# A decoder layer on one core: the convolution's inverse transform goes ahead of the out-projection's first products

## The chip, the cores and the metric

The kernel runs on one core of one Trainium2 chip. The core has a matrix engine (TensorE, PE in the profile), two engines for elementwise work (VectorE, DVE; ScalarE, ACT), a general one (GpSimd, POOL) and SyncE (SP), which here only starts transfers. Each engine works through its own queue in order; semaphores tie the queues together. Matrix products are written to PSUM, a small memory of eight banks; everything else lies in SBUF.

The metric is the device time of one execution, in microseconds (us). Three runs of the kernel before took 299.83, 300.6 and 301.85 us; the median is 300.6.

## What is computed

One decoder layer on 256 tokens of width 1024, in float32:

```python
h = rms_norm(x, norm1_g)
q, k, v, u = split(h @ w_in)                     # 512 columns each, u has 1024
q, k = rope(rms_norm(q)), rope(rms_norm(k))      # 8 heads of 64
attn = causal_softmax_attention(q, k, v)         # one block of 256 tokens, so plain causal attention
a, g = split(u + glu_b)
c = causal_depthwise_conv(a * sigmoid(g), 31 taps) + dw_b
conv = silu(layer_norm(c))                       # 512 channels
x = x + concat([attn, conv]) @ w_out             # the out-projection, 1024 x 1024
h = rms_norm(x, norm2_g)
x = x + (silu(h @ w_gate) * (h @ w_up)) @ w_down # the FFN, hidden width 2816
```

## The kernel before

**Split operands.** TensorE multiplies a rounded float32 type, so each operand is kept as two parts: hi (rounded) and lo (the rest). A product is three matmuls: hi with hi, hi with lo, lo with hi. In the names of the profile, `wh` and `wl` are hi and lo of weights, `mixh` and `mixl` of the out-projection's input, `yh` and `yl` of the convolution's spectrum. ScalarE makes each hi (a copy into the rounded type), and then VectorE makes the lo (source minus hi).

**The weights** stream in the order in which they are used, as 1 MB blocks (`raw`, four buffers), and are split in pieces of 128 x 1024, two to a block. There are seven buffers each of `wh` and `wl`. `feed(upto)` makes the hi part of pieces up to `upto + 1` and the lo part of those up to `upto`; when the lo of a block's second piece is issued, the load of the block four further on is issued on SP (L179). TensorE uses one piece for four products of the out-projection, so the hi of a piece is made five pieces ahead of its use and the lo four pieces ahead.

**The scheduler.** The order of work on each engine's queue is the order in which the Python program issues it, and a pass at the end fixes that order. Side work is written as generators ("tasks"). `spawn(gen, wait)` puts one on a list with a due time; `step()` runs every task that is due up to its next `yield n`, sets it due again n steps later, and moves the clock `now` on by one. In the input projection a step is made once for each of its 40 units of six matmuls. In the attention's output loop there is a step for every second head. In the out-projection and the FFN `product()` makes a step after each second product, that is after each six matmuls.

**The convolution** is done by a Fourier transform of length 288, as matrix products. A forward transform gives `hf`; VectorE multiplies by the taps' spectrum to get `Y` (three row groups: 128, 128 and 69 rows, the last row being the bias `dw_b`, written by a small DMA). `conv_task` splits `Y` into `yh`, `yl` (L183, L184). The inverse transform gives `cv`, for the two halves of the tokens: two banks of nine matmuls, with the three matmuls of a product at L215, L216 and L217. It is the first part of `ln_task`, and the rest of that task is the layer norm: statistics of `cv` (L559, L560) and `nb` (L564) on VectorE, one step later; `yn` (L569) on ScalarE, three steps after that; two steps after that eight transposes `cT` on TensorE (L580), SiLU to `cs` (L583), and the split of `cs` into rows 4 to 7 of `mixh` and `mixl`.

**The order around the change.** The attention's output loop issues the matmuls `O` (L625, L626) for eight heads. In its first step, `conv_task` issues the splits of `Y`. After heads 3 and 7 the loop issues the split of `O` into rows 0 to 3 of `mixh` and `mixl`. After the loop `ln_task` is spawned, due at once, which means at the next step. SP is given two loads of `x` for the residual (L635). Then come the out-projection's products for k = 0 to 3 (the attention's rows of `mix`; for each k, two token halves and two column halves, 16 products in four banks `po`), with a `feed` ahead of each k. The next 16 products use rows 4 to 7, the convolution's. They are ordered by column half, and each bank is then added to `x`, and transposed (`x2T`) and split for the FFN. The FFN's gate and up products are `fg`, its down products `pd`.

Of the kernel before, what the change touches and what calls it, by code (L numbers as in the profile page):

```python
# [121 lines left out]
def build(nc, tc, t):  # L122
    with ExitStack() as ctx:
        _build(nc, tc, t, ctx)
    keep_order(nc, tc)


def _build(nc, tc, t, ctx):
# [9 lines left out]
    def mm_bank(name, cols=512):  # L138
        return psum.tile([P, cols], F32, name=name, tag="mm", bufs=4)
# [21 lines left out]
    def step():  # L161
        for task in list(tasks):
            while task in tasks and task[0] <= now[0]:
                try:
                    task[0] = now[0] + next(task[1])
                except StopIteration:
                    tasks.remove(task)
        now[0] += 1
# [25 lines left out]
    def feed(upto):  # L194
        last = NB * BW // PIECE - 1
        while len(pieces) <= min(upto + 1, last):
            dst, src, j = new_piece()
            nc.scalar.activation(dst[0], src, AF.Copy)  # L198
            waiting.append((dst, src, j))
        while waiting and waiting[0][2] <= upto:  # L200
            dst, src, j = waiting.pop(0)
            if j >= 40 and j % 4 == 1:
                nc.scalar.activation(dst[1], dst[0].bitcast(F32), AF.Copy, scale=-1.0)  # L203
                nc.gpsimd.dma_start(dst[1].bitcast(F32), src, accum_op=ALU.add)  # L204
            else:
                nc.vector.tensor_tensor(dst[1], src, dst[0].bitcast(F32), op=ALU.subtract)  # L206
            if j % 2:
                load_block(j // 2 + RAW)

    def wtile(col, width):  # L210
        j, c = divmod(col, PIECE)
        return [p[:, c:c + width] for p in pieces[j]]
# [427 lines left out]
    def product(bank, lhs, w, start, stop):  # L640

        for a, (l, r) in enumerate(((lhs[0], w[0]), (lhs[0], w[1]), (lhs[1], w[0]))):
            nc.tensor.matmul(bank, l, r, start=start and a == 0, stop=stop and a == 2)  # L643
        ticks[0] += 1
        if ticks[0] % 2 == 0:
            step()
# [24 lines left out]
        yield 0  # L671

    off = 10 * BW
    for k in range(4):
        feed(off // PIECE + LEAD)
        for i in range(NT):
            for n in range(2):
                if k == 0:
                    po[i, n] = mm_bank(f"po{i}{n}")
                product(po[i, n], [m[:, k, tok(i)] for m in mix], wtile(off + n * W, W), k == 0, False)  # L680
        off += D
# [147 lines left out]
```

## Time and profile before

| | |
|---|---|
| median of three runs | 300.6 us (299.83 to 301.85) |
| the profiled execution | 301.44 us |
| its span, first to last instruction | 299.7 us |
| its mean granted TensorE clock | 0.994 |
| busy: TensorE / its weight loads | 293.0 / 237.2 us |
| busy: VectorE / ScalarE / GpSimd | 166.6 / 168.9 / 26.7 us |
| loaded and stored | 63.89 MB |

All times inside the execution are counted from the first instruction. In a line of the timeline, the first number is the start and the second the length. Then come the engine, the line of the kernel, the operation, output `<-` inputs, sizes and a count. A bracket gives the idle time of that engine before the instruction and what ended it. A matmul's length includes the time until its results have drained, so lengths of neighbours overlap; the distance from start to start is the cost of one in a row. "PEld" is the load of the stationary operand, which runs beside matmuls. The granted clock is the share of its full speed that TensorE was given.

### The profile page before, as it was taken

The page shows a single profiled execution, that of the slowest core. Times are in us where ns is not written, and L with a number is a line of the kernel's source. Part 1 is how long each engine was busy: PE and PEld are TensorE (multiplying, and loading weights), DVE is VectorE, ACT ScalarE, POOL GpSimd, SP SyncE. Part 2 cuts the span into 40 slices and gives each one's busy share as a digit, 9 for nine tenths or more (in the row PEclk, how much of TensorE's full clock was granted, in tenths as well). Part 3 has the DMA queues.
Part 4 walks back from the last instruction along what each step waited for, and adds up shares of the span by engine and source line. Part 5 has one row for each costly group of instructions (what it writes and reads, how often), then busy time and mean ns, then how long its engine had stood idle before and what let it go on. Part 6 is the DMA issues. An engine that isn't in the chain of part 4 may idle for free.

```text
span 299.7 us, 3659 instructions
## 1 busy us (share of the span) xinstructions
PE 293.0 (98%) x1357; PEld 237.2 (79%) x1357; DVE 166.6 (56%) x278; ACT 168.9 (56%) x246; POOL 26.7 (9%) x48
## 2 busy tenths in 40 slices
PE   8999999999799999999999999999999999999995
PEld 6888877777588788888888888888888888888883
DVE  3899986999745857952542542542542644224011
ACT  6776759899515766564654744744744735544200
POOL 0006380000000000001101101101101101101100
PEclk9999999999989999999999999999999999999999
DMA  7999869446505353465795794794695779663312
GB/s 261 415 413 356 316 248 332 143 140 196 228 0 229 116 218 140 142 281 116 256 323 113 263 328 97 269 326 98 271 316 116 270 215 257 245 195 70 71 38 102
DMA packets 12340, 63.89 MB, mean 213 GB/s; under 512 B 1633, under 2 KB 2241, under 8 KB 6562
## 3 DMA queue, kind: packets, MB, share of 16 engines
q1 hardware_dynamic: 9874, 54.86, 49.1%
q0 software_dynamic: 2304, 8.79, 14.6%
q8 instruction: 10, 0.16, 0.2%
q14 instruction: 8, 0.07, 0.1%
q10 hardware_dynamic: 144, 0.00, 0.0%
HBM read 55.26 MB, written 1.05 MB: 188 GB/s over the span
## 4 chain that ended last, share of the span: by engine, by line
PE 87%; DVE 9%; ACT 2%; DMA 1%; issue 0%; SPq 0%; DVEq 0%; ACTq 0%
PE fg L643 40%; PE pd L643 20%; PE p L604 12%; PE po L643 8%; DVE wl L206 3%; PE aT L728 2%; DVE p L473 1%; DMA Y<-dw_b 1%; PE warm L261 1%; DVE sm L456 1%; DVE yl L184 1%; PE cv L215 1%; PE cv L216 1%; PE cv L217 1%; PE x2T L665 1%; DVE ua L500 0%
## 5 line engine op out<-in xcount | busy, mean ns | idle before, releaser
L198 ACT ACTIVATE wh<-raw 128x1024 fp32r<-128x1024 f32 x90 | 93.5, 1055 | 53.0 <-PE fg L643 25.3
L206 DVE TENSOR_TENSOR wl<-raw,wh 128x1024 fp32r<-128x1024 f32 x76 | 91.4, 1222 | 41.2 <-ACT wh L198 41.2
L643 PE MATMUL fg<-wh,g 128*128 128x512 f32 x352 | 111.5, 392 | 0.0
L643 PEld LDWEIGHTS fg<-wh,g 128*128 128x128 f32 x352 | 66.1, 188 | 13.5
L643 PE MATMUL fg<-wl,g 128*128 128x512 f32 x176 | 68.6, 390 | 0.0
L643 PE MATMUL pd<-wh,act 128*128 128x512 f32 x176 | 54.8, 390 | 0.0
L643 PEld LDWEIGHTS pd<-wh,act 128*128 128x128 f32 x176 | 33.0, 188 | 6.8
L643 PEld LDWEIGHTS fg<-wl,g 128*128 128x128 f32 x176 | 33.1, 188 | 6.6
L643 PE MATMUL pd<-wl,act 128*128 128x512 f32 x88 | 34.2, 389 | 0.0
L604 PE MATMUL p<-wh,xh 128*128 128x512 f32 x80 | 32.9, 412 | 0.0
L204 POOL DMA_DIRECT2D wl<-raw x14 | 12.3, 876 | 222.5 <-DVE wl L206 89.8
L604 PE MATMUL p<-wh,xl 128*128 128x512 f32 x80 | 31.3, 391 | 0.0
L604 PE MATMUL p<-wl,xh 128*128 128x512 f32 x80 | 26.5, 392 | 0.0
L732 DVE TENSOR_TENSOR act<-aT,act 128x512 fp32r<-128x512 f32 (+1 forms) x12 | 7.8, 648 | 31.4 <-ACT act L730 31.4
L730 ACT ACTIVATE act<-aT 128x512 fp32r<-128x512 f32 (+1 forms) x12 | 6.8, 563 | 25.2 <-PE aT L728 25.2
L643 PEld LDWEIGHTS pd<-wl,act 128*128 128x128 f32 x88 | 16.5, 188 | 3.4
L604 PEld LDWEIGHTS p<-wh,xh 128*128 128x128 f32 x80 | 15.1, 189 | 3.7 <-issue 0.7
L604 PEld LDWEIGHTS p<-wh,xl 128*128 128x128 f32 x80 | 15.1, 189 | 3.1
L604 PEld LDWEIGHTS p<-wl,xh 128*128 128x128 f32 x80 | 15.1, 189 | 3.0
L721 DVE SCALAR_TENSOR_TENSOR ac<-fg,rstd,sf 128x512 f32<-128x512 f32 (+1 forms) x12 | 8.1, 707 | 12.2 <-PE fg L643 11.6
L203 ACT ACTIVATE wl<-wh 128x1024 fp32r<-128x1024 f32 x14 | 14.7, 1048 | 0.0
L643 PE MATMUL po<-wh,mixl 128*128 128x512 f32 x32 | 13.1, 408 | 1.3 <-DVE mixl L184 1.3
(139 smaller groups left out, 266.4 us busy)
## 6 DMA issues: line engine op xcount, KB each, us to landing
raw<-w SPq DMA_DIRECT2D x45, 1024.0 KB, 5.3
wl<-raw POOLq DMA_DIRECT2D x14, 512.0 KB, 4.6
first<-first SPq DMA_DIRECT2D x8, 384.0 KB, 5.8
xtok<-xtok SPq DMA_DIRECT2D x2, 512.0 KB, 9.1
x<-xtok SPq DMA_DIRECT2D x2, 512.0 KB, 6.8
out<-o SPq DMA_DIRECT2D x4, 256.0 KB, 2.0
inv<-inv POOLq DMA_DIRECT2D x1, 768.0 KB, 7.0
fwd<-fwd POOLq DMA_DIRECT2D x1, 648.0 KB, 4.2
```

The lines of the kernel that those rows point to most:

```text
L184: eng.tensor_tensor(dst[1], src, dst[0].bitcast(F32), op=ALU.subtract)
L198: nc.scalar.activation(dst[0], src, AF.Copy)
L203: nc.scalar.activation(dst[1], dst[0].bitcast(F32), AF.Copy, scale=-1.0)
L204: nc.gpsimd.dma_start(dst[1].bitcast(F32), src, accum_op=ALU.add)
L206: nc.vector.tensor_tensor(dst[1], src, dst[0].bitcast(F32), op=ALU.subtract)
L215: nc.tensor.matmul(out, lhs[0], rhs[0], start=start, stop=False)
L604: nc.tensor.matmul(banks[i], (xh, xh, xl)[a][:, kt, sls[i]], w[a % 2], start=kt == 0 and a == 0, stop=kt == KT - 1 and a == 2 - (order[-1] ...
L643: nc.tensor.matmul(bank, l, r, start=start and a == 0, stop=stop and a == 2)
L721: nc.vector.scalar_tensor_tensor(u[:, :width], banks[i][:, W - width:] if width < W else banks[i], ffn["r"][:, i:i + 1], ffn["s", c][i][:, ...
L728: nc.tensor.transpose(b[:, a, :], ups[i][:, a * P:(a + 1) * P], ident)
L730: nc.scalar.activation(hi, b[:, 0:nf, :], AF.Copy)
L732: nc.vector.tensor_tensor(lo, b[:, 0:nf, :], hi.bitcast(F32), op=ALU.subtract)
```

## The change

One call of `step()` is added ahead of the loop over the out-projection's first 16 products:

```diff
@@ -671,6 +671,7 @@
         yield 0
 
     off = 10 * BW
+    step()
     for k in range(4):
         feed(off // PIECE + LEAD)
         for i in range(NT):
```

`ln_task` is the task that is due there. Its first part, the 18 `cv` matmuls, is issued ahead of the first product instead of behind the second. As the steps after that stay where they are, each later part of the task is issued two products (six matmuls) earlier too: the statistics behind product 2 instead of 4, `yn` behind product 8 instead of 10, and `cT`, `cs` and the split of `cs` behind product 12 instead of 14. Relative to the weights' feeds, which stay at their products, `yn` is now issued ahead of the feed of k = 2 and the `cT` group ahead of the feed of k = 3; each stood behind that feed before.

## The prediction

> **What bounds the kernel now.** I read the page first: is one engine full, and does its clock hold?
>
> ```profile
> span 299.7 us, 3659 instructions
> ...
> PE 293.0 (98%) x1357; PEld 237.2 (79%) x1357; DVE 166.6 (56%) x278; ACT 168.9 (56%) x246; POOL 26.7 (9%) x48
> ...
> PEclk9999999999989999999999999999999999999999
> ```
>
> TensorE (PE) is busy for 98% of the span, and the granted clock dips in one slice of the 40, the twelfth (7.5 us each: 82.4 to 89.9 us). That dip is where the change works. Second, the chain of waits in order of time (start, length, what), around that place:
>
> ```profile
> 77.75 1.89 DVE yl L184 x3
> 79.64 0.61 DVE mixl L184
> 80.25 0.04 issue
> ...
> 87.23 8.17 PE po L643 x36
> 95.40 0.87 PE cT L580 x8
> 96.27 11.73 PE po L643 x48
> 108.01 0.87 PE x2T L665 x8
> 108.88 1.38 PE po L643 x6
> 110.26 4.08 PE fg L643 x18
> ...
> 244.23 51.72 PE pd L643 x228
> ```
>
> At 77.75 the chain leaves TensorE for VectorE (DVE): three subtractions for yl, one for mixl, and only then products. From 110 us to 296 us it is TensorE without a break, 0.227 us for a product's matmul (51.72 / 228, and 8.17 / 36). So whatever TensorE gains before 110.26 should arrive at the end undiminished, unless something feeding it is late. Third, the timeline of TensorE there (start, duration, and in brackets the idle time before and who ended it):
>
> ```profile
> 78.27 0.50 PE L643 MATMUL po<-wh,mixh 128*128 128x512 f32 x1 [0.48 <-ACT mixh L183]
> 78.61 0.40 PE L643 MATMUL po<-wl,mixh 128*128 128x512 f32 x1
> 80.29 0.50 PE L643 MATMUL po<-wh,mixl 128*128 128x512 f32 x1 [1.29 <-DVE mixl L184]
> ...
> 81.17 0.63 PE L643 MATMUL po<-wh,mixl 128*128 128x512 f32 x1
> ...
> 84.50 0.39 PE L216 MATMUL cv<-yl,inv 69*128 69x512 f32 x1
> ...
> 84.96 0.40 PE L215 MATMUL cv<-yh,inv 128*128 128x512 f32 x1
> ...
> 86.84 0.39 PE L217 MATMUL cv<-yh,inv 69*128 69x512 f32 x1
> 87.07 0.39 PE L643 MATMUL po<-wh,mixh 128*128 128x512 f32 x1
> ...
> 95.24 1.03 PE L580 MATMUL cT<-c_ident,yn 128*128 128x128 f32 x8
> ...
> 110.09 0.39 PE L643 MATMUL fg<-wh,g 128*128 128x512 f32 x1
> ```
>
> The attention's last matmul ends at 77.79 (78.27 less 0.48). The first product then waits for ScalarE's mixh, and its third matmul 1.29 us for VectorE's mixl. Then the rhythm is slow: 8 steps from 81.17 to 84.50 take 3.33 us, while the inverse transform's second half (84.96 to 87.07, 9 steps in 2.11) has 0.234 us each. The windows say why (window, its length, busy time of PE, PEld, DVE, ACT and POOL, granted clock, DMA share, GB/s):
>
> ```profile
> 80.00:81.00 1.00, 0.71 (x3) 0.63 (x4) 0.83 (x2) 0.00 (x0) 0.00 (x0) 0.99 0.05 20
> 81.00:82.00 1.00, 1.00 (x4) 0.72 (x3) 0.00 (x0) 0.00 (x0) 0.00 (x0) 0.50 0.00 0
> 84.00:85.00 1.00, 1.00 (x5) 0.78 (x5) 0.00 (x0) 0.00 (x0) 0.00 (x0) 0.80 0.00 0
> ```
>
> The granted clock is 0.50 from about 81.0 to 84.4, right behind the idle time. At 0.234 the 8 steps would take 1.87 us, so half clock costs 1.46.
>
> **The change, part by part.** No instruction is removed or added. One more scheduler step ahead of the products starts the layer-norm task at once: its 18 cv matmuls go ahead of the first two products (6 matmuls), and each later stage of the task (statistics, yn, the cT transposes, the split of cs) is issued two products earlier. The task issues no DMA, and nothing of it is on the queues of SP or POOL. The rows on VectorE and ScalarE that matter:
>
> ```profile
> 79.55 1.28 DVE L184 TENSOR_TENSOR mixl<-O,mixh 128x512 fp32r<-128x512 f32 x2
> 90.39 0.16 DVE L564 SCALAR_TENSOR_TENSOR nb<-mv,lr 128x2 f32<-128x2 f32 x1
> 90.47 3.49 DVE L206 TENSOR_TENSOR wl<-raw,wh 128x1024 fp32r<-128x1024 f32 x3
> 97.64 0.69 DVE L184 TENSOR_TENSOR mixl<-cs,mixh 128x512 fp32r<-128x512 f32 x1 [3.68 <-ACT mixh L183]
> 99.21 0.69 DVE L184 TENSOR_TENSOR mixl<-cs,mixh 128x512 fp32r<-128x512 f32 x1 [0.88 <-ACT mixh L183]
> 77.11 0.63 ACT L183 ACTIVATE yh<-Y 69x512 fp32r<-69x512 f32 x1 [0.34 <-DMA Y<-dw_b]
> 90.59 1.45 ACT L569 ACTIVATE yn<-cv,nb,lr 128x512 f32<-128x512 f32 x2 [0.89 <-DVE nb L564]
> ```
>
> *The new wait.* What feeds the inverse transform is ready before what feeds the products: on VectorE's queue the three yl stand ahead of mixl, in an order that the change leaves alone. They end at 78.38, 79.01 and 79.64 (thirds of the chain's 1.89). The first cv matmul needs only yh and can start at 77.79; the second needs the first yl: 78.38 + 0.04 (the issue row) = 78.42. The fifth needs the second yl, at 79.05, and comes at 78.42 + 3 x 0.234 = 79.12; the eighth needs the third, at 79.68, and comes at 79.83. So there is one wait, of 0.63 less the first matmul's own 0.23. Behind it on TensorE's queue stands everything else; nobody else waits for that. A step after a wait is longer once (78.27 to 78.61 is 0.34): +0.11.
>
> *The products.* 17 x 0.234 = 3.98 after 78.42, plus 0.11, puts the first product at 82.51. By then mixh and mixl of the attention (both ended by 80.83, 79.55 + 1.28) are long there, so the waits of 0.48 and 1.29 go. In the order of before, the inverse transform lay beside nothing; now it covers the split of the attention's output.
>
> *The clock.* In the 3.4 us before 81.0 TensorE was idle for 1.77 us. Now the idle time is about 0.4 us. I take full clock; the ends are 0 and 1.46 us of loss, and the row nearest to so short an idle time is 84.96 to 87.07, a stretch without waits at clock 1.00.
>
> *The second split.* The 48 products' matmuls from 96.27 take 11.73; at 0.227 they would take 10.90. The 0.83 over is where cT leaves only two products before the channels of cs are wanted: mixl comes 2.40 and 3.97 us after cT starts (97.64 and 99.21 against 95.24), and takes 0.69. With the transposes two products earlier, four products (12 x 0.227 = 2.72) and cT's own 0.87 lie between, so the first is wanted (by the third matmul of a product) 3.59 + 0.45 = 4.04 us after cT's start and is there at 3.09; the second is wanted two products on, at 5.40, and is there at 4.66. The 0.83 goes.
>
> *What is late next.* The last cv is 4.45 us earlier or a little more (82.3 against 86.84), so nb ends at about 86.1 and yn at 87.6; cT comes after 12 products, at 82.51 + 36 x 0.227 = 90.68. Spare: 3.1 us, about as before (95.24 less 92.04). On ScalarE yn now stands ahead of the hi copy of weight piece 27 and the cs group ahead of piece 28; on VectorE both cs mixl stand ahead of wl of piece 27, which so ends at 90.68 + 4.66 + 1.16 = 96.5 (it ended at 93.96). Product 27, its first reader, comes at 82.51 + 26 x 0.681 + 0.87 = 101.1: hidden with 4.6 to spare; if that cover went, each further us would be one of TensorE's.
>
> *Sum.* The first FFN matmul comes at 82.51 + 96 x 0.227 + 2 x 0.87 = 106.04, against 110.09: 4.05 us. By parts: 0.48 + 1.29 idle, 1.46 clock, 0.83 second split, and some 0.5 of longer steps at these waits and of matmul ends that are modelled late; less the new 0.5. The profiled execution took 301.44 (span 299.7), so it would take 297.4. It lies 0.84 above the median of 300.6. The three runs spread over 2.0 us (299.83 to 301.85), which is room for a half-clock stretch that some of them had and some not. Without that term the gain is 2.59. From the median that gives 296.6 with it and 298.0 without it; from the fastest run without it, 297.2. I take 297.3.
>
> **Rivals.**
>
> *The half clock stays.* It may come from something else than these waits, such as the load of the stretch before. Then the loss of 1.46 remains, and the time is 297.4 + 1.46 = 298.9. For it: neither gap alone reaches half of the 3.4 us that the slow stretch lasts. Against: the dip is the only one in the page's row, and starts 0.7 us after the only long gap. The Trainium skill (TensorE: Matmul & The Clock Gate, in "Why this matters for your kernels") lets throughput drop only after an idle gap of more than some 3 us; by that rule a gap of 1.29 us is not the cause, the loss stays, and the time is this rival's. The trace speaks against the rule as it stands: no gap of that length precedes the dip.
>
> *The wait is for the whole of yl.* If the transform waited for all three yl, it would start its second matmul at 79.68: 1.26 lost, 298.6, and 300.0 if that longer idle time halves the clock again. Against: the first product starts at 78.27, while ScalarE's second mixh still runs, so waits go by slices there.
>
> *The weights come late: slower.* The load into the next raw buffer waits for wl of piece 27.
>
> ```profile
> 93.99 0.33 SPq L179 DMA_DIRECT2D raw<-w  x1
> raw<-w SPq DMA_DIRECT2D x45, 1024.0 KB, 5.3
> ```
>
> It was issued at 93.99; now at 96.5, while TensorE is 4 us ahead, and lands 5.3 later, at 101.8. Its first piece (34) is copied when TensorE starts piece 29, four products into the FFN: 106.04 + 2.7 = 108.8. Spare 7 us. From there on each us late is one us of idle TensorE, as the four raw buffers pass a delay on. To end 1% slower it must eat 7 us of slack, the 4 us of gain and 3 us more: a landing of 19 us, which no weight row comes near.
>
> **How the numbers follow.** About 1% (3.0 us: below 297.6, above 303.6) is what a measurement of this kernel tells from no change. The forecast has 0.70, and its own range is 296.4 to 298.2, by whether the unprofiled runs held the half clock; 297.6 lies inside it, so some 0.70 of it counts as faster. The half clock stays: 0.14, within 1%. Whole yl: 0.10, mostly within 1%. Late weights: 0.03; anything else, evenly: 0.03. Faster 0.49 + 0.03, slower 0.04, within 1% the rest, 0.44. The range takes in the two middle rivals up to 299.3: 296.3 to 299.3.
>
> **What would show it.** On TensorE the 18 cv matmuls directly behind O, one idle time of about 0.4 us ended by yl, and the first product near 82.5 with no wait for mixl; granted clock 1.00 through 78 to 86; the 48 matmuls after cT in about 10.9; the first fg near 106.0; from there on the same rhythm, 186 us to the last pd. It is wrong if the clock drops there all the same, if the cv group starts only at 79.7, or if TensorE shows new idle time ended by wl, wh or a load after 106.

## The result

The changed kernel takes 297.68 us (median of five runs, 297.62 to 297.83). The kernel before, run beside it, takes 300.04 (five runs, 299.83 to 301.85). The ratio is 0.991, with a 95% interval of 0.988 to 0.994: 0.9% faster, a difference clear of noise and, by the ratio itself, just inside the bound of 1% (its interval reaches past that).

The page of the profile after (same rows as were read before):

```profile
span 295.9 us, 3660 instructions
...
PE 290.3 (98%) x1357; PEld 235.8 (80%) x1357; DVE 166.3 (56%) x278; ACT 168.6 (57%) x246; POOL 26.6 (9%) x48
...
PEclk9999999999999999999999999999999999999998
```

The dip of the granted clock in the twelfth slice is gone, and the span is 3.8 us shorter. The 8 in the last slice is a drop at 294.14 us, behind TensorE's last matmul (which starts at 291.75); it costs nothing. The timeline of TensorE around the change:

```profile
77.91 0.50 PE L215 MATMUL cv<-yh,inv 128*128 128x512 f32 x1
78.63 0.49 PE L216 MATMUL cv<-yl,inv 128*128 128x512 f32 x1 [0.22 <-DVE yl L184]
78.97 0.40 PE L217 MATMUL cv<-yh,inv 128*128 128x512 f32 x1
...
82.47 0.40 PE L217 MATMUL cv<-yh,inv 69*128 69x512 f32 x1
82.70 0.40 PE L643 MATMUL po<-wh,mixh 128*128 128x512 f32 x1
82.94 0.40 PE L643 MATMUL po<-wl,mixh 128*128 128x512 f32 x1
83.17 0.39 PE L643 MATMUL po<-wh,mixl 128*128 128x512 f32 x1
```

The inverse transform runs directly behind the attention's output, with one short wait for yl. The products follow in the full rhythm, and neither mixh nor mixl is waited for any more. The windows (same columns as before) have full clock where it was 0.50 and 0.80:

```profile
81.00:82.00 1.00, 1.00 (x6) 0.78 (x5) 0.77 (x2) 0.00 (x0) 0.00 (x0) 1.00 0.00 0
84.00:85.00 1.00, 1.00 (x7) 0.80 (x6) 0.83 (x6) 0.00 (x0) 0.00 (x0) 1.00 0.00 0
```

And the chain of waits, from the first products to the end:

```profile
82.86 8.18 PE po L643 x36
91.04 0.87 PE cT L580 x8
91.92 12.29 PE po L643 x54
104.21 0.87 PE x2T L665 x8
105.08 1.38 PE po L643 x6
106.46 4.08 PE fg L643 x18
...
240.43 51.72 PE pd L643 x228
```

The products behind cT are now 54 in 12.29 us, 0.228 each; before they were 48 in 11.73, 0.244 each. The FFN begins 3.80 us earlier (110.26 to 106.46), and the last stretch of pd as well (244.23 to 240.43). What was gained before the FFN arrived at the end whole.

The span of this one execution fell by 3.8 us, but the median by only 2.4. The rest of this document is mostly about that difference.

### The profile page after: what moved, and what is told of

Same layout as the page of the kernel before. It is cut to its first block, busy times and chain, and to the rows that moved or that the text cites. A ratio compares the mean times of both kernels' runs of the same rounds, so it can differ in the third digit from the quotient of the medians.

```text
span 295.9 us, 3660 instructions
## 1 busy us (share of the span) xinstructions
PE 290.3 (98%) x1357; PEld 235.8 (80%) x1357; DVE 166.3 (56%) x278; ACT 168.6 (57%) x246; POOL 26.6 (9%) x48
## 4 chain that ended last, share of the span: by engine, by line
PE 94%; DVE 2%; DMA 1%; issue 1%; ACT 0%
PE fg L643 41%; PE pd L643 20%; PE p L604 18%; PE po L643 7%; PE aT L729 2%; PE S L447 1%; DMA first<-first 1%; PE pT L477 1%; PE x2T L665 1%; PE cv L216 1%; DVE wl L206 1%; PE cv L217 0%; DVE yb L527 0%; DVE ya L526 0%; PE cv L215 0%
## 5 line engine op out<-in xcount | busy, mean ns | idle before, releaser
L643 PE MATMUL po<-wh,mixh 128*128 128x512 f32 x32 | 12.6, 395 | 0.0
```

## The experiments

**How the runs are grouped.** For each run there is its mean granted clock, TensorE's share of full speed over the whole execution. Here "full clock" means that no half-clock stretch shows in this mean, and "one stretch" that one of about 3.4 us does. A run of this length with one half-clock stretch of 3.4 us has a mean of about 0.994 (0.5 x 3.4 / 300 missing). The runs fall into distinct groups: 0.997 to 1.000 (full clock), 0.993 or 0.994 (one stretch), 0.989 (two). A drop behind the last matmul, as in the profile after (1.76 us of half clock, mean 0.997), can account for a mean slightly under 1 at no cost. The kernel before ran 61 times beside the experiments, on three chips:

| | full clock | one stretch |
|---|---|---|
| first chip | 14 runs, median 300.12 us | 9 runs, median 301.56 us |
| second chip | 12 runs, 299.79 us | 9 runs, 301.54 us |
| third chip | 10 runs, 300.19 us | 7 runs, 301.35 us |

So the stretch is there in 25 of 61 runs and costs 1.2 to 1.75 us. Below, each kernel is compared with the kernel before on its own chip, by the runs with full clock, unless it says otherwise.

**Is it the wait that halves the clock?** The kernel before, with work put into the wait:

```diff
     off = 10 * BW
+    filler = t_bank("filler")
+    for _ in range(18):
+        nc.tensor.matmul(filler[:, 0:T], zeros[:, 0:P], zeros, start=True, stop=True)
     for k in range(4):
```

> The kernel before, with 18 matmuls of zeros (128 x 256 moving, result unused) ahead of the first product, which occupy TensorE while it would wait for mixh and mixl. Theory, that idle time in that place sets the half clock: granted clock full in every run, and a time near the fastest runs of the kernel before, 299.8 to 300.0, with a spread of some tenths. Rival, that the half clock has another cause: still runs up to 301.5, and a granted clock of 0.50 after 81 us in the profile.

Measured: 300.17 us (12 runs, 299.90 to 300.61), all 12 with full clock. The timeline of TensorE in the profiled run:

```profile
78.05 2.14 PE L676 MATMUL filler<-zeros 128*128 128x256 bf16 x18
79.95 0.47 PE L643 MATMUL po<-wh,mixh 128*128 128x512 f32 x1
80.26 0.40 PE L643 MATMUL po<-wl,mixh 128*128 128x512 f32 x1
80.57 0.51 PE L643 MATMUL po<-wh,mixl 128*128 128x512 f32 x1
```

The products begin no earlier than before (the third matmul at 80.57, against 80.29). Nothing of the wait is gained; TensorE is only kept occupied. With that the half-clock runs disappear, and the time is that of the kernel before at full clock (300.12). The stretch came from the idle time in this place, and not from the load before it.

**The second split, from both sides.** First the changed kernel with only the cv matmuls moved, and the rest of the layer norm where it stood before; then the kernel before with only `cT`, `cs` and the split of `cs` moved two products earlier:

```diff
             cv.append(b)
-        yield 1
+        yield 2
```

> The changed kernel, with one step more between the inverse transform and the statistics, so that only the 18 cv matmuls are moved and the rest of the layer norm stands where it stood before (cT behind 14 products). Theory: the 0.83 us of waits for the split of cs come back: 297.7 + 0.8 = 298.5 us, clock full. Rival, that the second split cost nothing by its place: 297.7.

```diff
-LN_WAIT = 2
+LN_WAIT = 1
```

> The kernel before, with the wait ahead of cT one step shorter (cT behind 12 products) and cv where it was. Theory: the waits for the split of cs go and nothing else: 0.8 us under the kernel before, run for run, with the same half clock in some runs: 299.0 to 301.0. Rival, as above: no difference.

Measured: 298.54 us for the first (6 runs, 298.32 to 299.36, all with full clock). That is 1.58 under the kernel before on that chip. For the second 299.34 us in the 8 of 12 runs with full clock, 0.78 under it, and about 301.0 in the other 4. The chain of waits of the first:

```profile
92.48 0.87 PE cT L580 x8
93.35 11.69 PE po L643 x48
```

and of the second:

```profile
92.67 0.87 PE cT L580 x8
93.55 12.29 PE po L643 x54
```

With two products between cT and the first use of cs, the 48 matmuls take 11.69 (0.244 each); with four, 54 take 12.29 (0.228 each). The place of cT alone is worth 0.8 us, wherever cv stands. The two parts, 1.58 and 0.78, sum to 2.36. The changed kernel itself gains 2.14 and 2.36 on the two other chips (from its runs further down).

**How much idle time it takes.** The changed kernel three times with its one remaining wait lengthened, by additions on VectorE that nothing reads (n = 2, 4, 6), and once as it is. The edit with n = 2:

```diff
         G["ys"] = [(yh[:n, j, :], yl[:n, j, :]) for j, n in enumerate((P, P, R3))]
+        junk = early.tile([P, W], F32, name="junk")
+        for _ in range(2):
+            nc.vector.tensor_tensor(junk, Y[0], Y[1], op=ALU.add)
```

> The changed kernel itself, as the level for the three beside it: 297.7 us, spread of some tenths, full clock in every run. If its steadiness was chance, some runs lie 1.4 us higher with a lower mean clock.

> The changed kernel with two more subtractions' worth of work on VectorE (0.6 us each, result unused) ahead of yl, so that TensorE's one wait ahead of the second cv matmul grows by 1.2 us to some 1.7, all of it in one piece; that is about the sum of both waits of the kernel before. Theory, that the share of idle time within a stretch of some 3.4 us decides: 298.9 us, and in part of the runs half clock and 300.4. Rival, a gap must last above 3 us: 298.9 in every run, full clock.

> The same with four: the wait is some 2.9 us in one piece. Theory: 300.1 us, with half clock in most runs and then 301.6. Rival, above 3 us: 300.1 in every run, full clock.

> The same with six: the wait is some 4.1 us. Both: half clock in every run, or nearly, 301.3 + 1.5 = 302.8 us. If the clock stays full even here, the idle time of this place isn't what sets it: 301.3.

| kernel | idle time ahead of the second cv matmul (profiled run) | runs with one stretch | with two | median, or the groups (us) |
|---|---|---|---|---|
| changed kernel | 0.23 | 0 of 6 | 0 | 297.65 |
| n = 2 | 1.56 | 1 of 10 | 0 | 298.88 full clock, 300.41 the one |
| n = 4 | 3.02 | 7 of 12 | 4 | 300.15 the one at full clock; 301.66 to 302.35; 303.08 to 303.45 |
| n = 6 | 4.47 | 3 of 6 | 3 | 303.07 to 303.32; 303.69 to 304.80 |

The timeline with n = 4, around the wait, and then its windows:

```profile
78.29 0.50 PE L215 MATMUL cv<-yh,inv 128*128 128x512 f32 x1
81.80 0.64 PE L216 MATMUL cv<-yl,inv 128*128 128x512 f32 x1 [3.02 <-DVE yl L184]
```

```profile
81.00:82.00 1.00, 0.20 (x1) 0.20 (x2) 1.00 (x3) 0.00 (x0) 0.00 (x0) 1.00 0.03 8
82.00:83.00 1.00, 1.00 (x3) 0.79 (x3) 1.00 (x3) 0.00 (x0) 0.00 (x0) 0.51 0.00 0
84.00:85.00 1.00, 1.00 (x4) 0.81 (x3) 0.14 (x1) 0.00 (x0) 0.00 (x0) 0.50 0.00 0
85.00:86.00 1.00, 1.00 (x4) 0.79 (x4) 0.54 (x1) 0.00 (x0) 0.00 (x0) 0.79 0.00 0
```

The same picture as in the kernel before: half clock from about the end of the wait, for 3.4 us. With n = 6 the clock drops while TensorE is still waiting (windows of that kernel):

```profile
81.00:82.00 1.00, 0.00 (x0) 0.00 (x0) 0.97 (x2) 0.00 (x0) 0.00 (x0) 0.73 0.03 12
82.00:83.00 1.00, 0.07 (x1) 0.07 (x1) 1.00 (x3) 0.00 (x0) 0.00 (x0) 0.50 0.03 8
```

Half clock came without any gap of 3 us in the kernel before, 25 times in 61, and once with n = 2. The rival's plain form, a gap above 3 us, falls. My own form, the share of idle time, is not settled by n = 2: with 1.56 us in one piece I expected the stretch in part of the runs and got 1 of 10, against 9 of 21 of the kernel before on that chip. Ten runs don't hold these two shares clearly apart.

**A version beyond both.** What is left of the wait in the changed kernel comes from VectorE, where a weight piece's wl stands ahead of yl. In the attention's output loop the feed goes behind the step, in the changed kernel (two runs on different chips) and in the kernel before:

```diff
     for h in range(H):
-        feed(unit // 2 + LEAD)
         if h % 2 == 0:
             step()
+        feed(unit // 2 + LEAD)
```

> The changed kernel, with the feed in the attention's output loop issued behind the step instead of ahead of it, so that yl no longer stands behind a weight piece's wl on VectorE. Theory: the wait that is left ahead of the second cv matmul (78.63 against a start of 77.91) goes, 0.5 us: 297.2. If something else holds the first cv matmuls: 297.7.

> The changed kernel again, beside the next on the same chip: 297.7 us.

> The changed kernel with the feed behind the step in the attention's loop, again, for a direct comparison: 0.5 us under the changed kernel on the same chip, 297.2. If the earlier difference came from the chip alone: no difference.

> The kernel before with the feed behind the step, cv where it was. If the place of cv is what matters, this doesn't help there: mixh now stands behind a weight piece's wh on ScalarE and mixl behind its wl on VectorE, so the products wait longer: 300.3 us with full clock (0.4 over the kernel before), and half clock in at least as many runs. If an earlier yl is worth something by itself: 299.5.

Measured: 297.23 us on the first chip and 297.23 on the third (6 runs each, 296.84 to 297.94 over both, all 12 with full clock). The changed kernel beside it on the third chip takes 297.83 (6 runs, 297.30 to 297.98). The medians differ by 0.6, but the runs overlap, so a gain of that size is likely and not certain. The timeline of the second of these runs shows the wait gone:

```profile
77.83 0.51 PE L215 MATMUL cv<-yh,inv 128*128 128x512 f32 x1
78.17 0.39 PE L216 MATMUL cv<-yl,inv 128*128 128x512 f32 x1
78.40 0.40 PE L217 MATMUL cv<-yh,inv 128*128 128x512 f32 x1
```

In the kernel before the same edit gives 300.31 us at full clock (9 runs, against 300.19) and one stretch in 3 of 12. There it only moves the wait (timeline of TensorE):

```profile
79.27 0.50 PE L643 MATMUL po<-wh,mixh 128*128 128x512 f32 x1 [1.52 <-ACT mixh L183]
...
80.30 0.50 PE L643 MATMUL po<-wh,mixl 128*128 128x512 f32 x1 [0.30 <-DVE mixl L184]
```

This edit, and with it an earlier yl, shows a gain only where cv stands first.

## Why the prediction was right, point by point

- **The new wait.** Predicted one wait, for the first yl, with the second cv matmul at 78.42: it came at 78.63. Of the 0.21, 0.15 is that yl itself began at 77.90 in this execution, against 77.75. The first product was predicted at 82.51 and came at 82.70.
- **The products.** No wait for mixh or mixl is left. Moved alone, the cv matmuls gain 1.58 us at full clock; the sum left 1.76 for them (4.05 less the 1.46 of the clock and the 0.83 of the second split).
- **The second split.** Predicted 0.83; measured 0.78 by the kernel that has only this part, and about 0.8 in the changed kernel's own rows (0.244 against 0.228, times 48).
- **The clock.** Predicted 1.46 for the stretch, caused by the waits. The three chips show 1.44, 1.75 and 1.16 between the groups, and filling the wait removes it. The changed kernel, over the result and two repeats, has it in none of 17 runs.
- **The sum.** Predicted 4.05 for the profiled execution, measured 3.80 between the two executions (0.15 of the difference arose ahead of the change).
- **The time.** Predicted 297.3, measured 297.68, inside the narrower range of 296.4 to 298.2. I left it open whether the unprofiled runs had the stretch. Most have not: 36 of 61. The gain at full clock was put at 2.59, and is 2.36 between the medians of the result. My slightly greater chance went to a gain above 1% (0.52 against 0.44). That was the step that missed: I took 297.3, halfway between 296.6 with the clock term and 298.0 without it, though the three runs then known left room for a median that holds none of it. The median of before also came down with two more runs, from 300.6 to 300.04. So the forecast had a gain of 3.3 us from too high a level; the gain measured is 2.36. That the time came out 0.38 from the forecast, while the gain was 0.94 short, is partly luck: the two errors cancel in part.
- **The half clock stays:** refuted by the filled wait. The Trainium skill (TensorE: Matmul & The Clock Gate, "Why this matters for your kernels") asks for no idle gaps above some 3 us. Here that is not enough: the kernel before loses the clock in 25 of 61 runs, with gaps of 0.48 and 1.29 us in its profiled execution.
- **The wait is for the whole of yl:** refuted. The second cv matmul starts at 78.63, while the three yl last from 77.90 for 1.89 us, to 79.79 (timeline of VectorE after):

```profile
77.90 1.89 DVE L184 TENSOR_TENSOR yl<-Y,yh 128x512 fp32r<-128x512 f32 x3
...
94.86 0.69 DVE L184 TENSOR_TENSOR mixl<-cs,mixh 128x512 fp32r<-128x512 f32 x1 [0.88 <-ACT mixh L183]
95.47 3.49 DVE L206 TENSOR_TENSOR wl<-raw,wh 128x1024 fp32r<-128x1024 f32 x3
```

- **The weights come late:** the delay came as worked out, its consequence didn't. The wl of piece 27 went behind both mixl of cs (95.47, so done at about 96.6), and the load it releases was issued at 96.75 (predicted 96.5, before 93.99):

```profile
96.75 0.33 SPq L179 DMA_DIRECT2D raw<-w  x1
```

  The chain from 106.46 on is TensorE alone, in the same rhythm as before. No load and no split of weights appears in it. The slack of about 7 us was not measured by itself; no run pushed the load further.

## What to carry to other kernels

Where an engine in order waits, look at which of the queued groups has its inputs first, by the order on the engines that make them: here yl stood ahead of mixl, and one line put the readers in the same order. When a stage stands on a chain of other engines (cT, SiLU, split), count the work between its start and its first reader; four products covered what two did not. Before adding a clock term to a median, group the runs by their mean granted clock: a profiled execution may carry a loss that most runs don't have.

## What the runs showed that I had not expected

The length of the longest wait does not seem to decide by itself. The kernel before has 0.48 and 1.29 us, 1.77 in sum within 2.5 us, and loses the clock in 25 of 61 runs; 1.56 in one piece does it in 1 of 10, 3.02 in 11 of 12, and 4.47 in 6 of 6. Where it does, the stretch lasts some 3.4 us, or twice that: by the mean clock with n = 4 in 4 runs and with n = 6 in 3, of which one was profiled (81.45 to 88.28).

That fits a clock that is reviewed every 3.4 us, at times that aren't tied to the kernel, and is halved where about half of that time was idle. The idle times are here counted from start to start less 0.23 (as the profile's matmul ends are late by 0.16); an amount of some 1.8 us would then have to fall into one such period. For n = 4 (81.80 - 78.29 = 3.51, less 0.23, is 3.28 idle, in 3.4) this gives a chance of (3.4 + 3.28 - 2 x 1.8) / 3.4 = 0.9, as seen. For the kernel before, with 2.0 idle spread over 2.57 us (0.55 and 1.45; the last group of `O` is taken as 0.37 long, its distance to the first cv matmul in the changed kernel), a period must hold all but 0.2 of it, which gives 1 - 2.17 / 3.4 = 0.36, against 25 of 61. For n = 2 (1.83 idle) it is at the edge: about a half if the amount is just below 1.83, nothing if it is just above. This is an estimate fitted to four counts; which runs lose the clock was not controlled.

The periods themselves show in two traces (read from their windows, at ends of stretches and of the execution). In the kernel before the clock falls at 80.98 and, after the last matmul, again at 299.43; with n = 4 at 82.01 and 300.47. The distances are 218.45 and 218.46 us, 64 times 3.413, and each of the two stretches lasts 3.41. Counted back in the same way from the drop behind the last matmul, two profiled executions with full clock had at most 1.5 us (the kernel before with cT early) and 1.6 us (the kernel before with the feed behind the step) idle in one period around the waits; the kernel before had 2.0 in the period up to 80.98, and its clock fell. If there is one such amount, it lies between 1.6 and 2.0 by these three executions. What it takes to get full clock back was not tested: in the profiled run with n = 6 the clock stayed at half through a period with 1.5 us idle (81.45 to 82.93).
